# Two of the first loads go through the storing queue: a strided mean-subtract kernel with both DMA rings in use from the start

## Chip, cores and metric

The kernel runs on one core of one Trainium2 chip. The metric is device time in microseconds (us), the median of several executions. A profile's span is about 1.8 us shorter than the time of the same execution. "Fast" is the undisturbed state of a run. Tiles are counted from 0. Each of the two engines that issue transfers has a DMA queue of its own, here also called its ring. A packet is one entry of the profile's DMA records: one row of a tile on one of the core's 16 DMA engines, or a completion entry of 4 bytes. To land is to be complete, as the waiting engine sees it.

## The reference

The input is float32, 8 x 4096 x 2112. Each four consecutive rows are averaged, and the average is subtracted from each of the four.

```python
x_r = x.reshape(B, S // stride, stride, D)      # stride = 4
pooled = x_r.mean(axis=2)
upsampled = np.repeat(pooled, stride, axis=1)
return (x - upsampled).astype(np.float32)
```

Every byte is read once and written once: 276.8 MB in, 276.8 MB out. One group of four rows is contiguous (33,792 bytes), so a tile of 128 groups is 128 rows of 33,792 bytes, 4.3 MB, and there are 64 tiles.

## The kernel before

Tiles are loaded by SP (the loading queue), worked on in place by VectorE (DVE), and stored by ACT (the storing queue). Six tile buffers let loads run ahead and stores lag behind.

```python
STRIDE = 4
IO_BUFS = 6
# ... cut
    io_pool = ctx.enter_context(tc.tile_pool(name="io", bufs=IO_BUFS))
    sum_pool = ctx.enter_context(tc.tile_pool(name="sum", bufs=1))

    for g0 in range(0, G, P):
        gsz = min(P, G - g0)
        x_tile = io_pool.tile([P, W], mybir.dt.float32)
        nc.sync.dma_start(out=x_tile[:gsz], in_=xg[g0:g0 + gsz])
        rows = x_tile[:gsz].rearrange("p (f d) -> p f d", f=STRIDE)
        s = sum_pool.tile([P, D], mybir.dt.float32)
        nc.vector.tensor_add(out=s[:gsz], in0=rows[:, 0, :], in1=rows[:, 1, :])
        for f in range(2, STRIDE):
            nc.vector.tensor_add(out=s[:gsz], in0=s[:gsz], in1=rows[:, f, :])
        nc.vector.scalar_tensor_tensor(   # rows = s * (-1/4) + rows, s broadcast over the four
            ...)
        nc.scalar.dma_start(out=og[g0:g0 + gsz], in_=x_tile[:gsz])
```

Of the kernel before, what the change touches and what calls it, by code (L numbers as in the profile page):

```python
# [1 line left out]

# [4 lines left out]

STRIDE = 4
IO_BUFS = 6  # L10


@with_exitstack
def kernel(
    ctx: ExitStack,
    tc: tile.TileContext,
    x: bass.AP,
    out: bass.AP,
):



    nc = tc.nc
    B, S, D = x.shape
    P = nc.NUM_PARTITIONS
    assert S % STRIDE == 0
    G = (B * S) // STRIDE
    W = STRIDE * D

    xg = x.rearrange("b (g f) d -> (b g) (f d)", f=STRIDE)  # L30
    og = out.rearrange("b (g f) d -> (b g) (f d)", f=STRIDE)

    io_pool = ctx.enter_context(tc.tile_pool(name="io", bufs=IO_BUFS))
    sum_pool = ctx.enter_context(tc.tile_pool(name="sum", bufs=1))

    for g0 in range(0, G, P):
        gsz = min(P, G - g0)
        x_tile = io_pool.tile([P, W], mybir.dt.float32)
        nc.sync.dma_start(out=x_tile[:gsz], in_=xg[g0:g0 + gsz])

        rows = x_tile[:gsz].rearrange("p (f d) -> p f d", f=STRIDE)
        s = sum_pool.tile([P, D], mybir.dt.float32)
# [3 lines that stand above are left out]
        nc.vector.scalar_tensor_tensor(  # L46
            out=rows,
            in0=s[:gsz, None, :].to_broadcast([gsz, STRIDE, D]),
            scalar=-1.0 / STRIDE,
            in1=rows,  # L50
            op0=mybir.AluOpType.mult,
            op1=mybir.AluOpType.add,
        )
        nc.scalar.dma_start(out=og[g0:g0 + gsz], in_=x_tile[:gsz])


# [1 line left out]
_INS = ['x']  # L58
_OUTS = [((8, 4096, 2112), 'float32')]


# [23 lines left out]
```

## Time and profile before

| | before |
|---|---|
| time, median | 1286.51 us (3 runs, 1286.51 to 1286.68) |
| span of the profile | 1284.7 us |
| VectorE busy | 80% |
| loading queue + storing queue, share of the 16 DMA engines | 50.0% + 49.9% |
| median load / store, issue to landing | 59.6 us / 43.8 us |

Lines of the page of the kernel before. The row of digits gives the busy share of the DMA engines in 40 equal slices of the span, in tenths (9 is 90% or more). The queue lines give packets, megabytes and the share of the 16 DMA engines' span that the packets took; q1 is the loading queue (SP), q10 the storing queue (ACT). The group line gives busy time and mean duration, then the idle time ahead of the group and its cause. The last two lines give the median time from issue to landing.

```profile
span 1284.7 us, 674 instructions
...
DVE 1026.1 (80%) x256; POOL 0.2 (0%) x4
...
DMA  9999999999999999999999999999999999999998
...
DMA packets 18437, 553.70 MB, mean 431 GB/s; under 512 B 2048, under 2 KB 2048, under 8 KB 2048
...
q1 hardware_dynamic: 9216, 276.83, 50.0%
q10 hardware_dynamic: 9216, 276.83, 49.9%
...
L43 DVE TENSOR_TENSOR s<-x_tile 128x2112 f32<-128x2112 f32 x64 | 150.9, 2358 | 237.5 <-DMA x_tile<-in_x_dram 237.3
...
x_tile<-in_x_dram SPq DMA_DIRECT2D x64, 4224.0 KB, 59.6
out_dram<-x_tile ACTq DMA_DIRECT2D x64, 4224.0 KB, 43.8
```

Two readings. First, the queues' shares sum to 99.9%, and no slice but the last is under 9: the DMA engines are never without a packet for long. VectorE, at 80%, waits 237 us for loads: it follows. Second, a load takes 59.6 us to land although a tile alone needs only 10 us (8 row packets of 1.25 us on each engine), and 20 us while loads and stores alternate: about three loads stand in the loading ring, and about two stores in the storing ring.

Stretches of the kernel before: VectorE busy, POOL busy, clock, DMA share, GB/s. The shares of short stretches are rough, as packets of 1.25 us straddle their edges, so a value can be a little over 1.

```profile
core 0: us, DVE busy (x) POOL busy (x), PEclk, DMA share, GB/s
...
8.00:13.00 5.00, 0.00 (x0) 0.00 (x0) 1.00 1.00 433
...
80.00:100.00 20.00, 19.79 (x7) 0.00 (x0) 1.00 1.00 433
```

At 8 to 13 us only loads run, on one ring; at 80 to 100 us loads and stores run on two. The rate is the same, 433 GB/s.

The start of the kernel before in order of time: start, duration, engine, line, operation.

```profile
0.73 113.48 SPq L39 DMA_DIRECT2D x_tile<-in_x_dram  x10
13.05 2.36 DVE L43 TENSOR_TENSOR s<-x_tile 128x2112 f32<-128x2112 f32 x1 [13.05 <-DMA x_tile<-in_x_dram]
...
29.22 101.04 ACTq L54 DMA_DIRECT2D out_dram<-x_tile  x7
```

The storing queue does nothing until 29.22 us. That is what the change wants to use.

### The profile page before, as it was taken

How to read it: one execution, taken by the hardware profiler on the slowest of the kernel's cores; microseconds unless marked ns; L12 is line 12 of the kernel's file. 1: busy time of each engine (PE TensorE's matmuls, PEld its weight loads, DVE VectorE, ACT ScalarE, POOL GpSimd, SP SyncE). 2: the span in 40 equal slices, each digit the busy share in tenths (PEclk: the TensorE clock that was granted, in tenths of full speed). 3: DMA queues.
4: the chain of work that ended last, by engine and by line, in shares of the span. 5: the costliest groups of instructions: out<-in, count | busy, mean ns of one | idle time of the engine just before them, and what ended most of it. 6: DMA issues, size and time to landing. Idle time of an engine off the chain costs nothing.

```text
span 1284.7 us, 674 instructions
## 1 busy us (share of the span) xinstructions
DVE 1026.1 (80%) x256; POOL 0.2 (0%) x4
## 2 busy tenths in 40 slices
DVE  5998778787787877878778787787887878778784
POOL 0000000000000000000000000000000000000000
DMA  9999999999999999999999999999999999999998
GB/s 404 421 438 438 433 425 437 438 427 432 437 437 426 435 437 431 429 437 437 431 428 438 437 431 429 437 436 432 428 438 436 430 430 437 437 426 433 438 431 380
DMA packets 18437, 553.70 MB, mean 431 GB/s; under 512 B 2048, under 2 KB 2048, under 8 KB 2048
## 3 DMA queue, kind: packets, MB, share of 16 engines
q1 hardware_dynamic: 9216, 276.83, 50.0%
q10 hardware_dynamic: 9216, 276.83, 49.9%
q14 instruction: 5, 0.04, 0.0%
HBM read 276.82 MB, written 276.82 MB: 431 GB/s over the span
## 4 chain that ended last, share of the span: by engine, by line
DVE 80%; another core or an unknown queue 17%; DMA 1%; issue 1%; DVEq 0%
DVE x_tile L46 45%; DVE s L45 24%; DVE s L43 12%; DMA x_tile<-in_x_dram 1%; DVEq L43 0%
## 5 line engine op out<-in xcount | busy, mean ns | idle before, releaser
L46 DVE SCALAR_TENSOR_TENSOR x_tile<-s,x_tile 128x8448 f32<-128x8448 f32 x64 | 573.3, 8958 | 2.2
L43 DVE TENSOR_TENSOR s<-x_tile 128x2112 f32<-128x2112 f32 x64 | 150.9, 2358 | 237.5 <-DMA x_tile<-in_x_dram 237.3
L45 DVE TENSOR_TENSOR s<-s,x_tile 128x2112 f32<-128x2112 f32 x128 | 301.8, 2358 | 4.4
L69 POOL MEMSET const-bfloat16-1.0<- 128x1 bf16 x1 | 0.1, 103 | 0.0
L69 POOL MEMSET const-uint8-127<- 128x1 uint8 x1 | 0.1, 102 | 0.0
L69 POOL MEMSET const-float32-0.0<- 128x1 f32 x1 | 0.1, 100 | 0.2 <-issue 0.2
L69 POOL MEMSET const-float32-1.0<- 128x1 f32 x1 | 0.1, 99 | 0.0
## 6 DMA issues: line engine op xcount, KB each, us to landing
x_tile<-in_x_dram SPq DMA_DIRECT2D x64, 4224.0 KB, 59.6
out_dram<-x_tile ACTq DMA_DIRECT2D x64, 4224.0 KB, 43.8
```

The source lines that it names most:

```text
L43: nc.vector.tensor_add(out=s[:gsz], in0=rows[:, 0, :], in1=rows[:, 1, :])
L45: nc.vector.tensor_add(out=s[:gsz], in0=s[:gsz], in1=rows[:, f, :])
L46: nc.vector.scalar_tensor_tensor(out=rows, in0=s[:gsz, None, :].to_broadcast([gsz, STRIDE, D]), scalar=-1.0 / STRIDE, in1=rows, op0=mybir. ...
L69: nc = _bacc.Bacc("TRN2", target_bir_lowering=False, num_devices=1)
```

## The change

The second and the fourth tile (tiles 1 and 3) are loaded through ACT's queue, so that both rings hold loads from the beginning.

```diff
+SHARED = (1, 3)
...
-        nc.sync.dma_start(out=x_tile[:gsz], in_=xg[g0:g0 + gsz])
+        first = g0 // P in SHARED
+        loader = nc.scalar if first else nc.sync
+        loader.dma_start(out=x_tile[:gsz], in_=xg[g0:g0 + gsz])
```

In the source, the load of tile 1 stands behind the store of tile 0 on the same engine, which waits for VectorE. Whether ACT meets them in that order is up to the framework that schedules the program.

## The prediction

> **What bounds the kernel.** The DMA engines, from first packet to last. The page's queue table gives the loading queue 50.0% and the storing queue 49.9% of the 16 engines' span: 99.9% of 1284.7 us. So one 33,792-byte row packet takes 0.50 x 1284.7 x 16 / 8192 = 1.25 us on its engine, and one 4.3 MB tile takes 8 x 1.25 = 10 us alone, 20 us when load and store alternate. 128 transfers need 1281 us; the other 4 us are the first packet's latency and the last receipt. VectorE is busy 80% and waits for loads (237 us in the chain of waits): it follows.
>
> **Does one ring leave bandwidth unused at the start?** That is the change's hope. The stretches say no: with the loading queue alone (8 to 13 us) 433 GB/s at DMA share 1.00, with both queues (80 to 100 us) the same. This agrees with the Trainium skill, "DMA: Bandwidth & Descriptors", section "Issuing engines are not separate DMA queues": all issuers end on the same 16 engines. The second ring can't add bytes per second.
>
> **What the change moves.** No bytes, no vector work. Two load issues (0.33 us each) go from SP to ACT; neither is critical. I expect the scheduler to place both ACT loads ahead of the first store, as their buffers are free at time 0. Then:
> - Tiles 0 and 1 arrive together. The engines alternate between rings, so tile 0 lands after 15 packets, not 8: VectorE's first add starts at about 21.7 us, not 13.05.
> - VectorE needs 16.17 us a tile and works without a wait until about 183 us (tile 10), instead of catching up at 110 us. The first store is issued at 38 us, not 29.2.
> - The engines always have queued packets: at 38 us part of tile 3's load and tiles 4 and 5 still wait.
> - Afterwards the six buffers are shared out differently: about two loads and three stores queued instead of three and two. Median load, issue to landing, drops from 59.6 to about 40 us; the store's rises from 43.8 to 61-64 us.
> - At the end VectorE is done earlier (about 1259 us, now 1270), but the stores wait as one longer queue; the last packet ends at the same time. Before, the last store's issue at 1270.3 came just as the preceding store ran out, so there is nothing to win there either: some tenths of a us at most.
>
> On the critical path: nothing. Predicted 1286.5 us.
>
> **Chance of slower.** If ACT keeps program order, load 1 stands behind store 0's wait. It then starts only near 53 us, lands near 65-73, VectorE idles about 36 us, and the DMA engines run empty for 20 to 25 us in all, an estimate from the same durations: 1307 to 1311 us, still within 2%. I give this one in ten.
>
> **What shows it right or wrong.** Right: queue shares sum to 99.9%; 62 loads issued by SP, 66 transfers by ACT; all slices of DMA at 9; first vector add near 21.7 us; landing medians 40 and 62 us. Wrong: a slice of DMA below 9 in the first four, ACT's loads issued after 29 us, VectorE waiting tens of us before tile 1 or 3.
>
> **What would make it wrong.** The order on ACT; buffers handed out so that tile 3 comes late; a semaphore shared by a load and a store that makes SP or ACT wait and leaves the rings empty; stores queued so deep that loads starve.
>
> Range: 1285.0 to 1289.5 us. Faster by over 2%: 0.01; within 2%: 0.95; slower: 0.04.

## The result, and the profile after

| | before | after |
|---|---|---|
| time, median of 6 | 1286.53 us | 1286.78 us |
| range | 1286.44 to 1286.84 | 1286.48 to 1287.03 |
| profiled span | 1284.7 us | 1285.2 us |
| first VectorE instruction that waits for a tile | 13.05 us | 23.08 us |
| last store issued | 1270.3 us | 1260.8 us |

The ratio is 1.0001, 95% interval 0.9988 to 1.0014: the same. (A ratio here is the mean time of one kernel's fast runs over that of the other's of the same rounds, so it is not quite the ratio of the medians quoted.)

Lines of the page after the change.

```profile
span 1285.2 us, 673 instructions
...
DVE 1026.1 (80%) x256; POOL 0.2 (0%) x4
...
DMA  9999999999999999999999999999999999999998
...
DMA packets 18437, 553.70 MB, mean 431 GB/s; under 512 B 2048, under 2 KB 2048, under 8 KB 2048
...
q10 hardware_dynamic: 9504, 285.48, 51.5%
q1 hardware_dynamic: 8928, 268.18, 48.4%
...
L46 DVE TENSOR_TENSOR s<-x_tile 128x2112 f32<-128x2112 f32 x64 | 150.9, 2358 | 228.0 <-DMA x_tile<-in_x_dram 227.7
...
out_dram<-x_tile ACTq DMA_DIRECT2D x64, 4224.0 KB, 63.8
x_tile<-in_x_dram SPq DMA_DIRECT2D x62, 4224.0 KB, 39.7
x_tile<-in_x_dram ACTq DMA_DIRECT2D x2, 4224.0 KB, 32.4
```

Part of the share moved from one queue to the other, and the two still sum to 99.9%. The median load lands 20 us sooner after its issue, the median store 20 us later: one queued load has become one queued store.

Stretches after the change.

```profile
core 0: us, DVE busy (x) POOL busy (x), PEclk, DMA share, GB/s
...
8.00:13.00 5.00, 0.00 (x0) 0.00 (x0) 1.00 1.00 433
...
80.00:100.00 20.00, 19.86 (x5) 0.00 (x0) 1.00 1.00 433
```

At 8 to 13 us two rings now carry loads, and the rate is 433 GB/s as before.

The start after the change, in order of time.

```profile
0.73 0.89 ACTq L42 DMA_DIRECT2D x_tile<-in_x_dram  x2
0.73 183.51 SPq L42 DMA_DIRECT2D x_tile<-in_x_dram  x11
23.08 2.36 DVE L46 TENSOR_TENSOR s<-x_tile 128x2112 f32<-128x2112 f32 x1 [23.08 <-DMA x_tile<-in_x_dram]
...
39.24 145.90 ACTq L57 DMA_DIRECT2D out_dram<-x_tile  x10
```

Both ACT loads were issued within 0.73 to 1.62 us, ahead of the first store: the scheduler did not keep the order of the source. Tile 0 shared the engines with tile 1, so VectorE started 10 us later. That delay cost nothing that can be told from noise, and the experiments ask why.

### The profile page after: what moved, and what is told of

Same layout as the page of the kernel before. It is cut to its first block, busy times and chain, and to the rows that moved or that the text cites. A ratio compares the mean times of both kernels' runs of the same rounds, so it can differ in the third digit from the quotient of the medians.

```text
span 1285.2 us, 673 instructions
## 1 busy us (share of the span) xinstructions
DVE 1026.1 (80%) x256; POOL 0.2 (0%) x4
## 4 chain that ended last, share of the span: by engine, by line
another core or an unknown queue 78%; DVE 10%; DMA 9%; SPq 1%; issue 0%; DVEq 0%
DVE x_tile L49 6%; DMA x_tile<-in_x_dram 5%; DMA out_dram<-x_tile 4%; DVE s L48 3%; DVE s L46 1%; SPq L42 1%; DVEq L46 0%
## 6 DMA issues: line engine op xcount, KB each, us to landing
out_dram<-x_tile ACTq DMA_DIRECT2D x64, 4224.0 KB, 63.8
x_tile<-in_x_dram SPq DMA_DIRECT2D x62, 4224.0 KB, 39.7
```

## The experiments

**Theory A**: the DMA engines are full, so the time is the packets' time plus the time in which the engines are empty. An order matters only if it empties them, and deep queues keep it from doing so. **Theory B**: two rings do move more at the start, and the gain was lost again through tile 0's later arrival. **Theory C**: the start or the tail has slack in any case. **Theory D**: the exchange is forgotten after the start.

### 1. Loads alone, on one ring and on two

Everything but the loads is cut, with one store at the end, so the result is wrong.

```diff
-        nc.sync.dma_start(...)  # and all vector work and stores
+        loader = nc.sync                                        # loads_one
+        loader = nc.scalar if g0 // P % 2 else nc.sync          # loads_two
+        loader.dma_start(out=x_tile[:gsz], in_=xg[g0:g0 + gsz])
+    nc.scalar.dma_start(out=og[G - P:G], in_=x_tile[:])         # once, after the loop
```

> Wrong result on purpose: the 64 loads alone, all on the loading queue, then one store of the last tile. Theory A (the DMA engines are already full with one ring): 64 x 8 packets x 1.25 us = 641 us, plus the lone store and the latencies, about 14 to 18 us: 654 to 660 us, the loading queue at 433 GB/s in the middle. Theory B (one ring leaves bandwidth unused; the second gives it, and the change lost that gain again through tile 0's later arrival): slower than loads_two by over 1%.

> Wrong result on purpose: the same 64 loads, alternately on the loading and the storing queue. Theory A: within 1.5 us of loads_one, the two queues at half each and 433 GB/s together. Theory B: shorter than loads_one by over 1% (over 6 us).

Measured: 658.3 us on one ring, 658.25 us on two (4 runs each, all within 0.3 us). The queue line and one stretch of the profile with one ring, then with two:

```profile
q1 hardware_dynamic: 9216, 276.83, 98.0%
...
100.00:600.00 500.00, 0.00 (x0) 1.00 1.00 432
```

```profile
q10 hardware_dynamic: 4752, 142.74, 50.5%
q1 hardware_dynamic: 4608, 138.41, 49.1%
...
100.00:600.00 500.00, 0.00 (x0) 1.00 1.00 432
```

One ring keeps a packet on the 16 engines for 500 us without a break, and a second ring halves the share of the first and adds nothing. (That the engines are full means this much: they always have a packet. Why a row packet takes 1.25 us, whether by the engine or by the memory behind it, no run here tests.) The first half of theory B falls: there was no gain to lose.

### 2. Less vector work

The second and third add are removed, so that VectorE needs 11.4 us a tile instead of 16.2; the result is wrong.

```diff
-        for f in range(2, STRIDE):
-            nc.vector.tensor_add(out=s[:gsz], in0=s[:gsz], in1=rows[:, f, :])
```

> Wrong result on purpose: the kernel before without its second and third add, so VectorE works 11.4 us a tile, not 16.2. Theory A: VectorE is not on the path, 1286 to 1287 us.

> Wrong result on purpose: the same cut of the changed kernel. Theory A: 1286 to 1287.5 us, the same as cut_before within 0.1%. Theory B (the change gains at the start and gives it back because VectorE starts 10 us later and is then behind until 185 us): with VectorE no longer behind, the gain shows, 3 to 10 us faster than cut_before.

Measured: 1285.89 us without the change, 1285.64 us with it. VectorE's line without the change, then with it:

```profile
DVE 724.2 (56%) x128; POOL 0.2 (0%) x4
```

```profile
DVE 724.3 (56%) x128; POOL 0.2 (0%) x4
```

VectorE's work fell from 1026 to 724 us and the time by less than 1 us, which is inside the interval of each ratio to the kernel before (0.9978 to 1.0011, and 0.9978 to 1.0008). The gain of 3 to 10 us that theory B expects is absent. VectorE is off the path in both.

### 3. The two loads kept behind the stores

This is the change in the order of its source.

```diff
-        loader.dma_start(out=x_tile[:gsz], in_=xg[g0:g0 + gsz])
+        load = loader.dma_start(out=x_tile[:gsz], in_=xg[g0:g0 + gsz])
+        if first:
+            tc.keep_in_program_order(load)
```

> The change with its two loads kept in program order on ACT, so that they stand behind the stores' waits. Theory A: the engines run empty, 20 to 25 us in all, so 1307 to 1311 us; a hole in the DMA line within the first 150 us and VectorE idle before tiles 1 and 3. If the start of the kernel had slack that hides an order (theory C: the first 150 us don't matter as the steady state catches up), it stays within 3 us of 1286.5.

Measured: 1324.15 us (1323.17 to 1324.55), ratio 1.0292, interval 1.0276 to 1.0307. The start of this kernel in order of time:

```profile
29.29 0.38 ACTq L59 DMA_DIRECT2D out_dram<-x_tile  x1
29.70 0.46 ACTq L42 DMA_DIRECT2D x_tile<-in_x_dram  x1
70.32 2.36 DVE L48 TENSOR_TENSOR s<-x_tile 128x2112 f32<-128x2112 f32 x1 [41.05 <-DMA x_tile<-in_x_dram]
...
103.02 0.46 ACTq L42 DMA_DIRECT2D x_tile<-in_x_dram  x1
138.54 2.36 DVE L48 TENSOR_TENSOR s<-x_tile 128x2112 f32<-128x2112 f32 x1 [35.91 <-DMA x_tile<-in_x_dram]
```

VectorE waits 41 us for tile 1 and 36 us for tile 3. While it works on tile 1, one load alone would have a buffer, that of tile 3, and it stands on ACT behind the stores of tiles 1 and 2 (it is issued at 103.02 us). While it works on tile 3, all six buffers are full. So nothing is queued, and the engines stand still. Its stretches and queue lines (the kernel before has a DMA share of 1.03 and 1.00 in the same two stretches):

```profile
q10 hardware_dynamic: 9504, 285.48, 50.1%
q1 hardware_dynamic: 8928, 268.18, 47.4%
...
74.00:87.00 13.00, 12.90 (x4) 0.00 (x0) 1.00 0.00 0
...
140.00:155.00 15.00, 14.86 (x5) 0.00 (x0) 1.00 0.02 7
```

The sum closes. Packets took 97.5% of 1321.4 us, 1288 us, where before they took 99.9% of 1284.7 us, 1283 us. So 5 us went into longer packets. The engines were empty for 33 us instead of 1 us. By the packet records two holes of 13.7 us, 73.6 to 87.3 us and 141.8 to 155.5 us, make up 27 us of that, and two of 1.4 us, one after each, another 3 us. Together with the longer packets this is the 36.7 us by which the span grew. Theory A holds and theory C falls for the start. The size was missed, though: 20 to 25 us were expected, 38 us came. The times of tile 1 were right: its load was to start near 53 us and to land within 65 to 73, and its first packet starts at 53.2 us and VectorE resumes at 70. What was too small is the empty time; which of its parts the estimate had short is not on record.

### 4. More vector work on the last tile alone

```diff
+        if g0 + P >= G:
+            for _ in range(1):            # 2 in tail2_after
+                nc.vector.scalar_tensor_tensor(
+                    out=rows, in0=s[:gsz, None, :].to_broadcast([gsz, STRIDE, D]),
+                    scalar=0.0, in1=rows,
+                    op0=mybir.AluOpType.mult, op1=mybir.AluOpType.add)
         nc.scalar.dma_start(out=og[g0:g0 + gsz], in_=x_tile[:gsz])
```

> The kernel before, with one more vector instruction of 8.96 us on the last tile alone (adds zero times the sum, result unchanged). Theory A: before the change the last store is issued just as the preceding one runs out, so nearly all of it shows: +8 to +9 us, 1294.5 to 1295.5 us. If the tail has slack in both (theory C): unchanged.

> The changed kernel with the same extra instruction. Theory A: the change turned one queued load into a queued store, VectorE ends 9.5 us earlier at the tail, so 8.96 us more of it cost at most 0.7 us: 1286.5 to 1287.5 us. Theory D (the change did nothing but exchange two issues; the order of the start is forgotten later): +8 to +9 us as in tail1_before.

> The changed kernel with two of them, 17.9 us. Theory A: about 10 us of slack are used up and the rest shows: +7.5 to +9 us, 1294 to 1296 us. Theory D: +17 to +18 us.

| extra VectorE work on the last tile | kernel before | changed kernel |
|---|---|---|
| none | 1286.50 us | 1286.78 us (from the rounds of the result, not these) |
| 8.96 us | 1293.57 us | 1286.46 us |
| 17.9 us | not run | 1292.18 us |

The tail of the kernel before with one extra instruction, then of the changed kernel with one:

```profile
1270.00:1275.00 5.00, 4.96 (x2) 0.00 (x0) 1.00 0.16 68
1275.00:1280.00 5.00, 4.68 (x1) 0.00 (x0) 1.00 0.00 0
1280.00:1285.00 5.00, 0.00 (x0) 0.00 (x0) 1.00 1.01 433
```

```profile
1270.00:1275.00 5.00, 0.00 (x0) 0.00 (x0) 1.00 1.00 433
1275.00:1280.00 5.00, 0.00 (x0) 0.00 (x0) 1.00 1.00 433
1280.00:1285.00 5.00, 0.00 (x0) 0.00 (x0) 1.00 0.16 68
```

The same instruction empties the engines for about 9 us (a mean over the 16; all of them at once are empty for 6.5 us, 1274.0 to 1280.6) in one kernel and not at all in the other. Of 8.96 us, 7.1 us showed without the change (1293.57 less 1286.50; the interval of the ratio, 1.0039 to 1.0069, leaves out 1) and nothing with it. So the kernel before had 1.9 us of slack at its tail and the changed one, by the second dose (17.9 us less the 5.7 us between 1292.18 and 1286.46), 12.2 us. Theory D falls: the exchange made at the start is still there 1200 us later, as one store more and one load fewer in the queues. It pays nothing here, since no slack was missing. Both doses that showed cost less than the least expected, by 0.9 us (tail1_before) and 1.8 us (tail2_after). The packet records of the kernel before show why for the first: the last store's packets start at 1271.2 us, but some engine is busy with the preceding store until 1272.4, and the last packet ends 12.4 us after the first. In the run with one extra instruction all engines were free, and the store took 10.2 us (1280.6 to 1290.8). The engines do not finish together, and waiting lets the late ones catch up.

### 5. Fewer buffers

```diff
-IO_BUFS = 6
+IO_BUFS = 3        # and SHARED = (1,) in bufs3_after; IO_BUFS = 4 in the other pair
```

> The kernel before with three tile buffers, not six. Theory A: the engines run empty for about 6 us more at the start and the end, 1291 to 1295 us.

> Three buffers, with the second tile loaded through the storing queue (the fourth has no free buffer at the start). Theory A: what hides tile 0's later arrival is the depth of the queues; with three buffers the engines run empty while VectorE works on it, 8 us more than bufs3_before: 1299 to 1303 us. Theory B or C: within 2 us of bufs3_before, or faster.

> The kernel before with four tile buffers. Theory A by packet arithmetic: 4 us of empty engines, 1288 to 1290 us. After the miss with three buffers, where single packets also took longer, I allow 1288 to 1297 us, with less scatter between runs than with three.

> The changed kernel with four tile buffers: all four first loads still go out at time 0, two on each ring. Theory A by packet arithmetic: when tiles 0 and 1 and then 2 and 3 have landed, at 43 us, store 0 has been queued since 39 us, so no hole opens; within 2 us of bufs4_before. If the depth of the queues (six buffers) is what hides tile 0's later arrival already here, it is 5 to 10 us slower than bufs4_before.

| buffers | without the change | with it |
|---|---|---|
| 6 | 1286.53 us | 1286.78 us |
| 4 | 1290.46 us (1290.3 to 1290.97) | 1292.06 us (1291.33 to 1292.99) |
| 3 | 1338.05 us (1316.83 to 1344.86; three of four runs are slow) | 1343.97 us (1336.22 to 1348.43) |

With four buffers both agree with what was expected, 4 us for the depth and 1.6 us for the change. The 1.6 us are small: the four runs of each kernel don't overlap, but the intervals of their ratios to six buffers do (1.0014 to 1.0047 and 1.0028 to 1.0058). A small hole did open with the change, against the wording of the expectation. This is the stretch from 45 to 60 us without the change, then with it:

```profile
45.00:60.00 15.00, 14.86 (x5) 0.00 (x0) 1.00 1.02 428
```

```profile
45.00:60.00 15.00, 14.90 (x4) 0.00 (x0) 1.00 0.91 351
```

By the packet records the hole lasts from 53.5 to 54.9 us, 1.4 us, and it accounts for most of the 1.6 us.

With three buffers the expectation of 1291 to 1303 us was far off in both kernels. The expected hole is there. This is the stretch in which VectorE works on tile 0, in the changed kernel with three buffers, after its queue lines:

```profile
q10 hardware_dynamic: 9360, 281.15, 50.1%
q1 hardware_dynamic: 9072, 272.50, 48.3%
...
32.00:40.00 8.00, 7.97 (x2) 0.00 (x0) 1.00 0.00 0
```

By the packet records the engines are empty from 32.8 to 40.2 us, 7.4 us, as theory A says; without the change there is no such hole. But what the change costs in total at this depth can't be read: runs of one kernel scatter over 12 to 28 us, and only one run without the change is fast. The profiles don't settle it either: by the queues' shares the engines are empty for about 20 us in all without the change (a slow run) and 21 us with it, so the hole does not show in the sum. Nor is the hole the main part of the time. Packets took 98.4% of 1334.4 us in this profile, 1313 us, where 1283 us do with six buffers: about 30 us are packets that lasted longer than 1.25 us, up to 2.5 us each. They are not spread evenly. A transfer has eight rows on each engine; of the 469 row packets of loads that took over 1.4 us, 299 lie among the first or the last of the eight, and of the 384 of stores none lies among the last three. In the run of experiment 3, with six buffers, nearly all of the long packets lie in the first 265 us, to some 100 us after the second hole (the kernel before has 45, 40 of them in its first 64 us). So packets are seen to lengthen in the runs in which the queues run short; by what mechanism, no run here tells, and it stays open.

No version with a right result beat the kernel before by more than the noise. The sum says why: 1281 us of packets at their usual 1.25 us, and some 4 us beside them, of which 1.7 us lie before the first row packet and 1.2 us after the last packet. The change, which moves two loads to the other queue, left the shares at 99.9%. An order that empties the engines adds to the sum, and it can lengthen packets too (5 us in experiment 3).

## Why the prediction was right, point by point

- **The bound.** Right. The engines are full; taking 302 us of work from VectorE moved the time by less than 1 us.
- **"The second ring can't add bytes per second."** Right, and shown directly: 658.3 us and 658.25 us. The Trainium skill, "DMA: Bandwidth & Descriptors", section "Issuing engines are not separate DMA queues", says that all issuers end on the same 16 engines.
- **The order on ACT.** Right: both loads within 0.73 to 1.62 us, the first store at 39.24 us (predicted 38).
- **First add at 21.7 us.** Measured 23.08. The mis-sized term is the landing of tile 0. The packet records show what was left out:

```
                 tile 0: last row packet ends   its sixteen 4-byte packets start   first add
before                 12.68 us                        12.34 to 12.68 us             13.05 us
after                  21.39 us                        22.32 to 22.63 us             23.08 us
```

  Each span runs from the first of the 16 engines to the last, and the row's end is that of the last. Before, an engine writes its 4-byte completion packet as soon as its last row is through. After, a row packet of the other ring comes in between: on the first engine the last row of tile 0 ends at 21.08 us, a row of tile 1 lasts from 21.08 to 22.33, and the completion packet follows. The same skill page, section "Why a DMA increments its semaphore by 16 and not by 1", says that each engine's last descriptor is the increment of the semaphore. In the records it comes after the other ring's turn, as a row would, and here that cost one more row packet, 1.25 us.
- **VectorE without a wait until tile 10.** Right: tile 10 starts at 184.81 us without a wait (predicted 183), and its waits fell from 59 to 54.
- **The buffers shared out differently.** Right: 39.7 and 63.8 us against 40 and 61 to 64. Experiment 4 shows that this lasts to the end; the last store is issued at 1260.8 us (VectorE's end was predicted near 1259).
- **The sign "all slices of DMA at 9".** All but the last, which is 8, as it is without the change.
- **The tail.** Right that nothing is gained; "some tenths of a us at most" of slack before was 1.9 us.
- **The chance of slower.** The step "If ACT keeps program order [...] 1307 to 1311 us, still within 2%" was wrong. Program order costs 2.9% (1324.15 us). The term that was mis-sized is the time with empty engines: 33 us, not 20 to 25 us, with 5 us of longer packets on top, which the prediction did not have. The whole verdict therefore rested on the order that the scheduler chose, more than the prediction said.

## What to carry to other kernels

When the shares of the DMA queues sum to the whole span, ask of a change whether it takes bytes away, empties the engines or lengthens the packets; which ring carried a transfer did not matter here. Moving a load to an engine that also issues stores did no harm where the load was issued ahead of the stores' waits and cost 2.9% where it was not, so look up that order in the compiled program or the trace. Depth hides late arrivals: with six buffers a first tile that is 10 us late cost nothing that can be told from noise, with four about 1.6 us in all, and a reordering at the start can change for good how many loads and stores are queued, which shows only when the tail has no slack left.

## What the Trainium skill lacked or had wrong

- "DMA: Bandwidth & Descriptors", section "Where 436 GB/s comes from", says that for transfers between HBM and SBUF the HBM side, about 358 GB/s, binds. With one core at work it did not: 432 to 433 GB/s in the full stretches shown, loads alone or loads and stores, which is near the 435 of the same section's other limit. The condition that the sentence leaves out stands higher on the page, section "Measured (HBM→SBUF, 128 partitions, SWDGE, issued from GpSimd)": about 358 GB/s is what each core gets when both cores of the HBM domain stream.
- The same page, section "Queues, rings and completion order", gives round-robin between rings by packets, and here rings with row packets of 33,792 bytes do share half and half. It says too that the semaphore increment lands only after every earlier write of its engine, across its queues, but not what a second ring so adds to a landing: here one row of the other ring, 21.08 to 22.32 us on the first engine, where the completion packet follows at once with one ring. Whether the turn or the ordering of writes holds it back, no run here separates.
- No page says that packets lengthen where queues run short. With three buffers about 30 us more than with six went into packets that took up to 2.5 us instead of 1.25 us. The cause is open.
